# Updating the recurrent states of eight samples in three GpSimd operations in place of ScalarE and VectorE

## The chip, the core and the metric

The kernel runs on one core of one Trainium2 chip. The metric is device time in microseconds (us) of one execution. Before the change it is 1835.34 us, the median of three runs (1832.19 to 1837.56). Five engines work at once, each through its own instructions in order: TensorE (PE in the profile; PEld is its weight loading), VectorE (DVE), ScalarE (ACT), GpSimd (POOL) and SyncE (SP). DMAs are issued by SP, ACT and POOL and move data beside them.

## The reference

One layer of a decoder is computed for a prompt of 256 tokens and for eight single new tokens (the "samples"), which stand together as 264 columns. It has a mixer of three branches (spatial gating, HGRN2 and GLA), an output projection and an MLP, in float32. What the change touches is the recurrence of the two linear-attention branches, for a sample a single step:

```python
S = exp(log_f) * S + k v^T      # per sample and head
o = S^T q
```

HGRN2 has 8 heads with states of 128x128, GLA 4 heads with states of 128x256, and each of the eight samples has states of its own, read from memory, updated, used for `o` and written back as outputs.

## The kernel before

All large matrix products go through the same stream. A weight block of four k-tiles by 256 columns (a "granule", 512 KB) is loaded by a DMA on SP's queue into `raw`; in two halves of 128x512 ScalarE rounds it into `whi` (line 109) and VectorE takes the remainder `wlo = raw - whi` (line 106); PE then runs three products for each 128x128 tile (lines 659, 660 and 661: high weights with high and low inputs, low weights with high inputs). `whi` and `wlo` have six buffers each, which is the granule in work and two ahead. PE's list therefore needs two halves of ScalarE's and of VectorE's work for each granule, and both engines can run a little ahead of it.

Everything else of the mixers is written as generators that are advanced a little after each granule (`background`). The order of PE's, POOL's (and, in part of the program, SP's) instructions is that of the program text; VectorE's and ScalarE's orders are put together by a planner when the program is built.

The sample states are the work of `samples_r`, called once for each of three groups: two halves of HGRN2 (group 0 and 1, four heads each, one step for each sample, so 8 steps) and GLA (group 2, two heads to a step, so 16 steps). The 32 steps lie between 357 and 817 us of the span. A step holds 128 partitions by 512 elements. In the loop over the steps n:

- POOL's queue issues the fetch of the state of step n+2 (line 1077, tile `st`, four buffers) and the fetch of the values v of step n+1, spread over all partitions (line 1083, tile `vbc`, two buffers).
- ScalarE multiplies the state by the decay, one head at a time because the factor is a value for each partition and head (line 1103).
- VectorE adds k times v, again one head at a time (line 1105).
- POOL's queue issues the store of the new state (line 1106).
- Once all heads of a sample are there, PE forms `o` from the states (line 686) at a later place in its list; this is also what frees the `st` buffers, so a fetch waits for PE's use of the state two steps back.

Two other items share POOL's queue: line 1134 writes the values of a group to memory before its steps, and line 1254 stores the prompt's final states when VectorE has them ready.

Of the kernel before, what the change touches and what calls it, by code (L numbers as in the profile page):

```python
# [10 lines left out]
AF = mybir.ActivationFunctionType  # L11
ALU = mybir.AluOpType
# [3 lines left out]
P = 128  # L16
D = 2048
KT = D // P
NP = 256
# [38 lines left out]
def hybrid_step_kernel(  # L58
# [8 lines left out]
    nc = tc.nc  # L67
    V, S, T = nc.vector, nc.scalar, nc.tensor
# [17 lines left out]
    def blk(shape=None, dt=F32):  # L86
        shape = shape or [P, 4, NT]
        return blkp.tile(shape, dt, tag="b", name=nm("b"))
# [4 lines left out]
    def tmp(shape, tag, bufs=2):  # L93
        return tp.tile(shape, F32, tag=tag, name=nm(tag), bufs=bufs)
# [4 lines left out]
    def mul(o, a, b):  # L99
        V.tensor_tensor(o, a, b, op=ALU.mult)  # L100
# [106 lines left out]
    def rstd_small(ms, scale, out):  # L207

        n, w = out.shape
        xx, aa = tmp([P, 16], "sx")[0:n, 0:w], tmp([P, 16], "sa")[0:n, 0:w]  # L210
        c = 0
        for m in ms if isinstance(ms, list) else [ms]:
            V.tensor_scalar(xx[:, c:c + m.shape[1]], m, scale, EPS, ALU.mult, ALU.add)
            c += m.shape[1]
        V.tensor_scalar(out.bitcast(I32), xx.bitcast(I32), -0.5, 1597463007.0, ALU.mult, ALU.add)
        for _ in range(3):
            mul(aa, out, out)
            V.scalar_tensor_tensor(aa, aa, -0.5, xx, ALU.mult, ALU.mult)
            V.scalar_tensor_tensor(out, aa, 1.5, out, ALU.add, ALU.mult)
# [842 lines left out]
    def samples_r(G):  # L1062

        dv = G.dv
        nj, nh = dv // P, 512 // dv
        q, k, g = G.q, G.k, G.g
        fs = tmp([P, 4, NS], "fs")
        S.activation(fs, g[:, :, NP:NT], AF.Exp)
        qm = blk([P, 4, NS, 32])
        mul(qm, q[:, :, NP:NT].unsqueeze(3).to_broadcast([P, 4, NS, 32]),  # L1070
            delta.rearrange("p (b c) -> p b c", b=NS).unsqueeze(1).to_broadcast([P, 4, NS, 32]))
        steps = [(b, h) for b in range(NS) for h in range(0, 4, nh)]
        ahead, vals = [], []

        def fetch(b, h):
            st = tmp([P, nh, dv], "st", ST_BUFS)
            nc.gpsimd.dma_start(st, G.s_in(b, h, nh))
            ahead.append((st, now[0]))

        def values(b, h):  # L1080
            v = tmp([P, 4, P], "vbc", VB_BUFS)
            r0 = 4 * nj * b + h * nj
            nc.gpsimd.dma_start(v, vs_d[G.i, r0:r0 + 4, :].partition_broadcast(P))
            vals.append((v.rearrange("p (h j) v -> p h (j v)", h=nh), now[0]))

        for s in steps[0:2]:
            fetch(*s)
            yield
        values(*steps[0])
        yield  # L1090
        os_ = tmp([P, dv], f"os{G.i}", 1)
        sts = []
        for n, (b, h0) in enumerate(steps):
            if n + 2 < len(steps):

                yield lambda: len(sts) + sum(len(x[3]) for x in samples) <= ST_BUFS - 3
                fetch(*steps[n + 2])
            if n + 1 < len(steps):
                values(*steps[n + 1])
            yield lambda: now[0] >= max(ahead[0][1] + FETCHED, vals[0][1] + FETCHED - 1)  # L1100
            st, v = ahead.pop(0)[0], vals.pop(0)[0]
            for i in range(nh):
                S.activation(st[:, i, :], st[:, i, :], AF.Copy, scale=fs[:, h0 + i, b:b + 1])  # L1103
            for i in range(nh):
                V.scalar_tensor_tensor(st[:, i, :], v[:, i, :], k[:, h0 + i, NP + b:NP + b + 1], st[:, i, :], ALU.mult, ALU.add)  # L1105
            nc.gpsimd.dma_start(G.s_out(b, h0, nh), st)  # L1106
            sts.append(st)
            if h0 + nh == 4:
                samples.append((now[0], (G, qm, os_), b, sts))
                sts = []  # L1110
            yield
        yield lambda: not samples
        yield READY
        ss, rr = tmp([P, 1], "sss", 1), tmp([P, 1], "srr", 1)
        S.activation(tmp([P, dv], "vt"), os_, AF.Square, accum_out=ss)
        rstd_small(ss, 1.0 / dv, rr)
        S.activation(os_, os_, AF.Copy, scale=rr)
        G.os = os_
        yield

    def mixer_r(G):
# [18 lines left out]
        q, k, g = G.q, G.k, G.g  # L1140

        bs.g.append(samples_r(G))


# [616 lines left out]
```

## Time and profile before

| | |
|---|---|
| median of three runs | 1835.34 us (1832.19 to 1837.56) |
| the profiled execution | 1832.18 us, of which the span of its instructions is 1830.4 us |
| PE busy | 1788.7 us, 98% of the span |
| PEld busy | 1696.5 us, 93% |
| VectorE busy | 1181.8 us, 65% |
| ScalarE busy | 1000.3 us, 55% |
| GpSimd busy, DMA issues counted | 131.3 us, 7% |
| ScalarE's part of the updates, line 1103 | 37.1 us in 96 instructions |
| VectorE's part of the updates, line 1105 | 34.2 us in 96 instructions |

A row of a group of instructions gives its line, its engine, what it writes and reads, how often, the busy time, the mean of one in nanoseconds, and behind the bar the time that the engine stood idle just before these instructions, with what ended it. A row of the timeline gives start, duration, engine and line, and in brackets the idle time before it. In a table of windows each row is a stretch of the span with the busy time of each engine in it. Matmuls are pipelined and the profile models their ends, so PE's busy share says little by itself; it is the idle time in front of PE's rows that tells where it had to wait.

### The profile page before, as it was taken

The numbers are of one execution on the slowest core, as the hardware profiler recorded it, in microseconds if no ns is written. First come the engines' busy times: TensorE is split into PE (matmuls) and PEld (weight loads), VectorE is DVE, ScalarE is ACT, GpSimd is POOL, SyncE is SP. The second block draws the span as 40 slices with busy tenths as digits, with TensorE's granted clock in tenths as the row PEclk, the third lists the DMA queues.
The fourth block names the chain that finished last, engine by engine and source line by source line (L and its number), as shares of the span: only waits on it lengthen the run. The fifth ranks groups of instructions, "written<-read, shape, count | busy, mean of one in ns | idle before, by whom it ended". The sixth has DMA issues, their size and how long they took to land.

```text
span 1830.4 us, 42186 instructions
## 1 busy us (share of the span) xinstructions
PE 1788.7 (98%) x17012; PEld 1696.5 (93%) x17012; DVE 1181.8 (65%) x2092; ACT 1000.3 (55%) x1818; POOL 131.3 (7%) x210
## 2 busy tenths in 40 slices
PE   6999999999999999999999999999999999999998
PEld 4889999989988999989999989999999999999997
DVE  4566677787576696566555667555666666666666
ACT  5544364666755765654445666555554545454544
POOL 4221000111111101210000000000000000000000
PEclk9999999999999999999999999999999999999999
DMA  9999697788787788897987964777666666666663
GB/s 326 354 343 304 195 304 231 215 266 276 239 287 233 229 270 278 274 323 250 308 254 265 327 180 146 246 256 227 191 197 194 197 194 196 195 195 196 196 196 106
DMA packets 330179, 442.05 MB, mean 242 GB/s; under 512 B 14946, under 2 KB 276944, under 8 KB 329984
## 3 DMA queue, kind: packets, MB, share of 16 engines
q1 hardware_dynamic: 311728, 380.26, 65.0%
q0 software_dynamic: 17184, 57.85, 9.1%
q8 instruction: 133, 2.18, 0.5%
q10 hardware_dynamic: 1072, 1.25, 0.2%
q14 instruction: 62, 0.51, 0.1%
HBM read 427.60 MB, written 11.70 MB: 240 GB/s over the span
## 4 chain that ended last, share of the span: by engine, by line
PE 88%; DMA 2%; DVE 2%; issue 1%; ACT 1%; POOL 0%; DVEq 0%; ACTq 0%; POOLq 0%
PE mm L659 27%; PE mm L661 26%; PE mm L660 26%; PE ada L376 3%; DMA vbc<-vs_d 1%; PE ada L308 1%; DVE wlo L106 1%; PE sm L851 1%; PE sm L1208 1%; PE sm L679 1%; PE sm L686 1%; DMA raw<-in_w_in_dram 0%; DVE b L106 0%; PE sm L1578 0%; ACT whi L109 0%
## 5 line engine op out<-in xcount | busy, mean ns | idle before, releaser
L659 PE MATMUL mm<-b,whi 128*128 128x264 f32 x4624 | 1292.4, 279 | 12.3 <-issue 5.1
L661 PE MATMUL mm<-b,wlo 128*128 128x264 f32 x4624 | 1279.7, 277 | 5.1 <-DVE wlo L106 4.5
L660 PE MATMUL mm<-b,whi 128*128 128x264 f32 x4624 | 1278.8, 277 | 0.8 <-DVE b L106 0.7
L106 DVE TENSOR_TENSOR wlo<-raw,whi 128x512 fp32r<-128x512 f32 x1136 | 774.4, 689 | 489.1 <-ACT whi L109 475.0
L109 ACT CAST whi<-raw 128x512 fp32r<-128x512 f32 x1136 | 691.8, 616 | 644.5 <-DVE wlo L106 331.7
L659 PEld LDWEIGHTS mm<-b,whi 128*128 128x128 f32 x4624 | 875.8, 189 | 53.0 <-issue 28.0
L661 PEld LDWEIGHTS mm<-b,wlo 128*128 128x128 f32 x4624 | 876.2, 189 | 7.3 <-DVE wlo L106 7.2
L660 PEld LDWEIGHTS mm<-b,whi 128*128 128x128 f32 x4624 | 876.2, 189 | 4.4 <-issue 3.0
L103 DVE TENSOR_TENSOR b<-b,mm 128x528 f32<-128x528 f32 (+1 forms) x137 | 95.7, 699 | 24.5 <-PE mm L661 13.0
L1105 DVE SCALAR_TENSOR_TENSOR st<-vbc,b,st 128x128 f32<-128x128 f32 (+1 forms) x96 | 34.2, 390 | 55.2 <-DMA vbc<-vs_d 50.4
L1103 ACT ACTIVATE st<-st,fs 128x128 f32<-128x128 f32 (+1 forms) x96 | 37.1, 430 | 50.5 <-DMA st<-in_state_hgrn_dram 26.9
L488 POOL DMA_DIRECT2D b<-in_w_ada_dram x64 | 46.2, 724 | 126.0 <-PE ada L308 94.4
L376 PE MATMUL ada<-araw,cT 128*32 128x512 f32 x296 | 39.8, 601 | 0.0
L308 PE MATMUL ada<-b,cT 128*32 128x256 f32 (+1 forms) x640 | 35.1, 356 | 2.8 <-DMA b<-in_w_ada_dram 2.6
L100 DVE TENSOR_TENSOR b<-b,b 128x512 f32<-128x512 f32 (+1 forms) x47 | 33.9, 741 | 1.3 <-ACT b L1221 1.0
L1106 POOL DMA_DIRECT2D out_dram<-st x32 | 23.6, 736 | 130.5 <-DVE st L1105 130.5
L308 PEld LDWEIGHTS ada<-b,cT 128*32 128x32 f32 x640 | 17.8, 113 | 14.9 <-DMA b<-in_w_ada_dram 6.2
L376 PE MATMUL ada<-b,cT 128*32 128x512 f32 x216 | 26.2, 594 | 0.0
L106 DVE TENSOR_TENSOR b<-gt,b 128x528 fp32r<-128x528 f32 x32 | 22.7, 710 | 3.2
L106 DVE TENSOR_TENSOR b<-b 128x1024 f32<-128x1024 f32 (+1 forms) x24 | 24.3, 1017 | 0.0
L1632 ACT ACTIVATE b<-vt 128x528 fp32r<-128x528 f32 x32 | 23.0, 719 | 1.0
L106 DVE TENSOR_TENSOR b<-b,b 128x1056 fp32r<-128x1056 f32 (+3 forms) x21 | 20.8, 991 | 4.0 <-ACT b L109 3.8
(344 smaller groups left out, 854.0 us busy)
## 6 DMA issues: line engine op xcount, KB each, us to landing
raw<-in_w_in_dram SPq DMA_DIRECT2D x231, 512.0 KB, 4.8
raw<-in_w_mlp_up_dram SPq DMA_DIRECT2D x128, 512.0 KB, 3.9
raw<-in_w_mlp_down_dram SPq DMA_DIRECT2D x128, 512.0 KB, 3.7
araw<-in_w_ada_dram SPq DMA_DIRECT2D x74, 512.0 KB, 5.7
b<-in_w_ada_dram SPq DMA_DIRECT2D x54, 512.0 KB, 6.6
b<-in_w_ada_dram POOLq DMA_DIRECT2D x48, 512.0 KB, 8.9
raw<-in_w_branch_dram SPq DMA_DIRECT2D x48, 512.0 KB, 4.5
raw<-in_w_out_dram SPq DMA_DIRECT2D x32, 512.0 KB, 5.3
```

The costliest lines, as they stand in the source:

```text
L100: V.tensor_tensor(o, a, b, op=ALU.mult)
L103: V.tensor_tensor(o, a, b, op=ALU.add)
L106: V.tensor_tensor(o, a, b, op=ALU.subtract)
L109: S.copy(hi, src)
L308: T.matmul(acc[32 * j:32 * j + 32, 0:n], cT[:, k, :], w[:, n * j:n * j + n], start=k == 0, stop=k == KT - 1)
L376: T.matmul(self.acc[32 * j:32 * j + 32, :], cT[:, k, :], ws[j // 2][:, j % 2 * 512:j % 2 * 512 + 512], start=k == 0, stop=k == KT - 1)
L488: queue.dma_start(w[:, i], w1[k * P:(k + 1) * P, :, self.k0 * P:(self.k0 + self.n) * P])
L659: T.matmul(o, a, xh(k + j), start=first and j == 0, stop=False)
L660: T.matmul(o, a, xl(k + j), start=False, stop=False)
L661: T.matmul(o, b, xh(k + j), start=False, stop=last and j == n - 1)
L1103: S.activation(st[:, i, :], st[:, i, :], AF.Copy, scale=fs[:, h0 + i, b:b + 1])
L1105: V.scalar_tensor_tensor(st[:, i, :], v[:, i, :], k[:, h0 + i, NP + b:NP + b + 1], st[:, i, :], ALU.mult, ALU.add)
```

## The change

The per-head loops on ScalarE and VectorE become three GpSimd operations over the whole step of 128x512: the state times the decay, the values times k (in place in `vbc`), and their sum into the state. The per-partition factors are read as operands spread along the free dimension. The fetches before and the store after them stay where they are in the text.

```diff
             st, v = ahead.pop(0)[0], vals.pop(0)[0]
-            for i in range(nh):
-                S.activation(st[:, i, :], st[:, i, :], AF.Copy, scale=fs[:, h0 + i, b:b + 1])
-            for i in range(nh):
-                V.scalar_tensor_tensor(st[:, i, :], v[:, i, :], k[:, h0 + i, NP + b:NP + b + 1], st[:, i, :], ALU.mult, ALU.add)
+            wide = [P, nh, dv]
+            nc.gpsimd.tensor_tensor(st, st, fs[:, h0:h0 + nh, b:b + 1].to_broadcast(wide), op=ALU.mult)
+            nc.gpsimd.tensor_tensor(v, v, k[:, h0:h0 + nh, NP + b:NP + b + 1].to_broadcast(wide), op=ALU.mult)
+            nc.gpsimd.tensor_tensor(st, st, v, op=ALU.add)
             nc.gpsimd.dma_start(G.s_out(b, h0, nh), st)
             sts.append(st)
```

In the built program PE's list is the same, row for row. VectorE and ScalarE lose 96 instructions each and keep the rest nearly in the old order; POOL's list gains 96, and reads for each step: fetch of state n+2, fetch of values n+1, the three operations of step n, store of step n.

## The prediction

> **What bounds the kernel now.** I read the page's busy times and chain first, then the groups of the two lines that go.
>
> ```profile
> span 1830.4 us, 42186 instructions
> PE 1788.7 (98%) x17012; PEld 1696.5 (93%) x17012; DVE 1181.8 (65%) x2092; ACT 1000.3 (55%) x1818; POOL 131.3 (7%) x210
> ...
> PE 88%; DMA 2%; DVE 2%; issue 1%; ACT 1%; POOL 0%; DVEq 0%; ACTq 0%; POOLq 0%
> ...
> L106 DVE TENSOR_TENSOR wlo<-raw,whi 128x512 fp32r<-128x512 f32 x1136 | 774.4, 689 | 489.1 <-ACT whi L109 475.0
> ...
> L1105 DVE SCALAR_TENSOR_TENSOR st<-vbc,b,st 128x128 f32<-128x128 f32 (+1 forms) x96 | 34.2, 390 | 55.2 <-DMA vbc<-vs_d 50.4
> L1103 ACT ACTIVATE st<-st,fs 128x128 f32<-128x128 f32 (+1 forms) x96 | 37.1, 430 | 50.5 <-DMA st<-in_state_hgrn_dram 26.9
> ```
>
> The chain that ended last is PE for 88%: its list of products sets the time. VectorE and ScalarE feed it with `wlo` and `whi`, and the lines that go are not on the chain. What they take is visible all the same: VectorE spends 34.2 us in line 1105 and stands 55.2 us in front of it, mostly for the values' DMA, with `wlo` instructions queued behind. So the question is what PE loses to late operands between 380 and 817 us. I cut that stretch where PE takes states or a group begins, and asked for each window's busy times; the last row is the sum over eleven adjoining windows.
>
> ```profile
> core 0: us, PE busy (x) PEld busy (x) DVE busy (x) ACT busy (x) POOL busy (x), PEclk, DMA share, GB/s
> ...
> 408.00:460.00 52.00, 52.00 (x591) 48.38 (x584) 38.48 (x76) 32.85 (x68) 10.20 (x15) 1.00 0.87 284
> ...
> 545.00:575.00 30.00, 26.90 (x405) 24.52 (x404) 22.45 (x46) 19.11 (x41) 5.72 (x9) 0.94 0.77 251
> ...
> 640.00:685.00 45.00, 42.80 (x594) 40.76 (x593) 40.56 (x65) 29.50 (x54) 4.96 (x8) 0.96 0.85 277
> 685.00:722.00 37.00, 37.00 (x449) 34.42 (x449) 28.18 (x50) 21.96 (x45) 7.97 (x12) 1.00 0.88 293
> ...
> 757.00:817.00 60.00, 57.31 (x514) 52.51 (x507) 35.11 (x71) 33.45 (x69) 13.99 (x21) 1.00 0.92 314
> sum 437.00, PE 426.42 PEld 395.58 DVE 303.82 ACT 276.69 POOL 66.18; mean PE 38.77 PEld 35.96 DVE 27.62 ACT 25.15 POOL 6.02
> ```
>
> PE is idle 10.6 us here (437.0 less 426.4). That is all that could be won in this stretch, 0.6% of the span.
>
> **The change part by part.**
>
> *What goes, and what it can win.* The timeline gives the places where PE waited for a `wlo`, and VectorE's wait just before each.
>
> ```profile
> 397.29 0.88 DVE L1105 SCALAR_TENSOR_TENSOR st<-vbc,b,st 128x128 f32<-128x128 f32 x3 [5.10 <-DMA vbc<-vs_d]
> ...
> 519.78 0.61 DVE L1105 SCALAR_TENSOR_TENSOR st<-vbc,b,st 128x128 f32<-128x128 f32 x2 [6.05 <-DMA vbc<-vs_d]
> ...
> 781.87 0.88 DVE L1105 SCALAR_TENSOR_TENSOR st<-vbc,b,st 128x256 f32<-128x256 f32 x2 [7.36 <-DMA vbc<-vs_d]
> ...
> 805.81 0.88 DVE L1105 SCALAR_TENSOR_TENSOR st<-vbc,b,st 128x256 f32<-128x256 f32 x2 [3.32 <-issue]
> ```
> ```profile
> 398.83 0.38 PE L661 MATMUL mm<-b,wlo 128*128 128x264 f32 x1 [0.53 <-DVE wlo L106]
> ...
> 521.67 0.38 PE L661 MATMUL mm<-b,wlo 128*128 128x264 f32 x1 [0.68 <-DVE wlo L106]
> ...
> 786.99 0.38 PE L661 MATMUL mm<-b,wlo 128*128 128x264 f32 x1 [0.43 <-DVE wlo L106]
> ...
> 807.34 0.38 PE L661 MATMUL mm<-b,wlo 128*128 128x264 f32 x1 [2.26 <-DVE wlo L106]
> ```
>
> VectorE stood 5 to 7 us three times for the values, and PE lost 0.5 to 0.7 us each time: the buffers ahead cover the rest. With lines 1103 and 1105 gone these three go: 0.53 + 0.68 + 0.43 = 1.6 us. The fourth, 2.26 us, stood behind a gap of VectorE that no DMA or engine ended, so I don't count it as won, but it may go too. Gain 1.6 us, with 0 and 10.6 us as ends. The 71 us of busy time that ScalarE and VectorE get back (37.1 + 34.2) win nothing beyond that, because PE is the bound.
>
> *What is added on POOL.* No row of before is a GpSimd operation of 128x512. The nearest are those of 128x128 and 128x32 around 1095 and 1101 us.
>
> ```profile
> 1094.89 0.44 POOL L1533 TENSOR_TENSOR gs<-gs,nr 128x128 f32<-128x128 f32 x1 [1.27 <-DVE nr L233]
> 1095.41 0.46 POOL L1534 TENSOR_TENSOR xsT<-xsT,gs 128x128 f32<-128x128 f32 x1
> ...
> 1100.13 0.25 POOL L1565 TENSOR_TENSOR b<-xsn,b 128x32 fp32r<-128x32 f32 x1
> ...
> 1100.81 0.21 POOL L1564 CAST b<-xsn 128x32 fp32r<-128x32 f32 x1
> ...
> 1101.30 0.47 POOL L1564 CAST b<-xsn 128x32 fp32r<-128x32 f32 x1
> ```
> ```profile
> 1101.28 0.43 DVE L106 TENSOR_TENSOR b<-vt,b 128x256 fp32r<-128x256 f32 x1 [0.50 <-ACT b L109]
> ```
>
> From 32 to 128 elements the time rises from 0.25 to 0.45 us, 2.1 ns an element, so 512 elements take 0.45 + 384 x 0.0021 = 1.25 us, and the start of the next comes 0.07 us after an end (1094.89 + 0.44 to 1095.41, rounded down). I use 1.31 us an operation and 3.94 us for the three of a step; over 32 steps that is 126 us of POOL. The floor of one operation is 0.45 us, that of a quarter of its size; the ceiling four of those, 1.8 us. I take the line between, because the three sizes lie on one.
>
> *What POOL and VectorE take from each other.* The cast of 128x32 takes 0.21 us, but 0.47 us where it starts 0.02 us behind a VectorE operation with two inputs, and it ends with that one (1101.77 against 1101.71 us). So the two engines don't run such work side by side. The Trainium skill, "SBUF — State Buffer", section "Who interferes with whom", says that a VectorE instruction with two SBUF inputs and a GpSimd instruction that reads SBUF exclude each other for the whole of the one that came first. By that rule the trace agrees in this one pair, 0.47 against 0.21 us; taken for every microsecond of POOL's work it makes the sum the upper end below, 8.8 us, and by what the trace shows of the cover ahead of PE it makes 1.6. The price for VectorE has two ends. It is nothing if `wlo` is far enough ahead, and at most the whole of POOL's time, if every microsecond of it stops VectorE. For the upper end I take each window's VectorE time, less line 1105, plus 3.94 us for each step that falls there.
>
> ```profile
> 408.00:460.00 52.00, 6.11 (x20) 1.00 0.87 284
> ...
> 545.00:575.00 30.00, 3.65 (x12) 0.94 0.77 251
> ...
> 640.00:685.00 45.00, 2.73 (x6) 0.96 0.85 277
> 685.00:722.00 37.00, 3.68 (x8) 1.00 0.88 293
> ...
> 757.00:817.00 60.00, 6.41 (x14) 1.00 0.92 314
> ```
>
> These rows are line 1105 alone. By POOL's new order the windows hold 6, 3, 2, 4 and 8 steps: 38.5 - 6.1 + 23.6 = 56.0 of 52 us; 22.5 - 3.7 + 11.8 = 30.6 of 30; 40.6 - 2.7 + 7.9 = 45.7 of 45; 28.2 - 3.7 + 15.8 = 40.3 of 37; 35.1 - 6.4 + 31.5 = 60.2 of 60. The excess is 4.0 + 0.6 + 0.7 + 3.3 + 0.2 = 8.8 us, and it would be PE's. But VectorE is only stopped while it has something to run, about three quarters of the time in the two worst windows (38.5 of 52, 28.2 of 37); with 0.75 of POOL's time they come to 50.1 of 52 and 36.3 of 37, and nothing is left over. For windows that full the row 640 to 685 is the nearest: VectorE is busy 40.6 of 45 us there and PE loses 2.2. I put 0.8 us on each of the two, 1.6 us together, between 0 and 8.8.
>
> *What now waits on POOL's queue.* The three operations of step n stand behind the fetch of n+2, which waits until PE has used a state two steps back; before, only DMAs stood there. ScalarE and VectorE did the update as soon as the data were in. So PE's wait for a state is new. The tightest places are the ends of group 0 and of group 2, where the last steps come in a row.
>
> ```profile
> 439.85 0.75 POOL L1077 DMA_DIRECT2D st<-in_state_hgrn_dram  x1 [11.35 <-PE sm L686]
> ...
> 790.61 0.72 POOL L1077 DMA_DIRECT2D st<-in_state_gla_dram  x1 [6.84 <-PE sm L686]
> 791.32 0.57 POOL L1083 DMA_DIRECT2D vbc<-vs_d  x1
> 791.88 0.71 POOL L1106 DMA_DIRECT2D out_dram<-st  x1
> ```
> ```profile
> 460.52 1.26 PE L686 MATMUL sm<-st,b 128*32 128x128 f32 x20
> ...
> 816.18 0.64 PE L686 MATMUL sm<-st,b 128*32 128x256 f32 x8
> ```
>
> With U for the three operations of a step: from 790.61 POOL issues a fetch and the values (to 791.9), then U, a store, a fetch and values (2.0), U, a store and values (1.3), U, a store (0.7), U: the last state is ready at 795.9 + 4U, and PE takes it at 816.18. So U may be 5.07 us. In group 0 the same sum from 439.85 (a fetch, values; U; store, values; U; store; U) gives 443.2 + 3U against 460.52, U up to 5.8 us. Alone U is 3.94; if each operation first waits for a whole `wlo` of 0.69 us it is 6.0. I let it wait for VectorE's busy share of the last window, 35.1 of 60: 0.59 x 0.69 = 0.41, so U = 5.17 and PE waits 4 x 0.10 = 0.4 us. The ends are 0 (U = 3.94) and 4 x 0.93 + 3 x 0.2 = 4.3 us. Other groups of steps have more room. Line 1254's store, which waits for VectorE, now holds updates up too; the next use is far enough off that I put nothing on it. The fetches issued behind an update leave up to 5 us later and are needed a whole step after that, and On SP's queue two weight loads change places with two others, which I put at nothing.
>
> *The sum.* Against the profiled execution's own 1832.18 us: -1.6 + 1.6 + 0.4 = +0.4, 1832.6 us. That execution lay 3.2 us under the median of the runs, 1835.34, so the median comes to 1835.7, say 1836 us: no change that this kernel's measurement can tell (0.3%, 5.5 us).
>
> **The rivals.**
>
> *Slower through VectorE.* POOL's 126 us stop VectorE whenever it holds the port; `wlo` comes late in the full windows, and PE waits for line 106. For it speaks the one pair of rows above, against it that waits of 5 to 7 us cost PE only 0.5 to 0.7. It decides when the stopped share of POOL's time passes about 0.83 (52 less 32.4, over 23.6). Price: the 8.8 us, without the 1.6 and with 0.4 for the states: 1835.3 + 7.6 = 1843 us.
>
> *Slower through the states.* POOL's operations take longer than the line through three small sizes gives, or VectorE always goes first, so that U is 7.4 us (1.31 plus 1.15 an operation, nearly two `wlo` each). PE waits 4 x 2.3 at 816 and 3 x 1.6 at 460, 14 us, and some less at other uses: 1835.3 + 14 = 1849 us, up to 1853. It decides from U = 5.07. The Trainium skill, "GPSIMD Engine Reference", section "Engine selection", advises VectorE for elementwise work because two-input operations are about twice as slow on GpSimd. No run here shows a GpSimd operation of this size yet.
>
> *Faster.* The waits for DMAs leave both feeding engines, the fourth `wlo` wait goes too, and the port costs nothing: -1.6 - 2.3, and some of the remaining 6.7 us of PE's idle time if its cause is a late `whi`: -4 to -8, 1828 to 1831 us. Against it: part of PE's idle time ends in nothing that the profile names.
>
> **How the numbers follow.** No change to tell: 0.42 (its own range 1830 to 1841). Slower through VectorE 0.23 and through the states 0.15, together 0.38. Faster by over 5.5 us: 0.20. The range of 1829 to 1850 us leaves out half of the faster case and the worst of the states case, some 0.2.
>
> **What would show it.** Lines 1103 to 1105 on POOL with about 1.3 us each, a little more where VectorE is busy. Line 106 with a mean above its 689 ns, or idle time before it, between 380 and 817 us. No wait of ScalarE or VectorE for `st` or `vbc`. PE's idle sum in these windows near 10.6 us; a wait of PE for POOL at the last line 686 of group 2, if anywhere. The prediction is wrong if operations of 128x512 take 2 us or more, if PE waits for line 106 for more than 5 us there, or if PE's idle sum halves.

## The result, and the profile after

The changed kernel takes 1841.88 us, the median of five runs (1839.12 to 1842.03), against 1833.96 us for the kernel before, also of five (1832.19 to 1837.56). The ratio is 1.0037 with a 95% interval of 1.0023 to 1.0051: slower by 7.9 us by the medians, by 6.8 us by the ratio. A few single executions of over 3100 us in the experiments below are left out of all medians and ratios, and from the one trace that was taken of such an execution, with twice GpSimd's reads, only GpSimd's own times are read. The time lies in the forecast's range (1829 to 1850 us), 5.9 us above its number and just outside the likeliest case's own range of 1830 to 1841. Nearest to it is the rival "slower through VectorE", 1843 us.

The page of the kernel after, its span, busy times and chain, and the groups that answer to those shown of before:

```profile
span 1837.3 us, 42020 instructions
PE 1789.7 (97%) x17012; PEld 1697.0 (92%) x17012; DVE 1235.9 (67%) x1996; ACT 973.3 (53%) x1722; POOL 264.2 (14%) x306
...
PE 89%; DVE 2%; ACT 1%; issue 1%; DVEq 0%; ACTq 0%
...
L106 DVE TENSOR_TENSOR wlo<-raw,whi 128x512 fp32r<-128x512 f32 x1136 | 827.0, 737 | 498.0 <-ACT whi L109 485.6
...
L1105 POOL TENSOR_TENSOR st<-st,vbc 128x512 f32<-128x512 f32 x32 | 51.9, 1620 | 2.5
L1103 POOL TENSOR_TENSOR st<-st,fs 128x512 f32<-128x512 f32 x32 | 43.5, 1361 | 20.7 <-ACT fs L1068 20.3
...
L1104 POOL TENSOR_TENSOR vbc<-vbc,b 128x512 f32<-128x512 f32 x32 | 37.5, 1173 | 2.2 <-DMA vbc<-vs_d 2.2
```

POOL works 132.9 us in the three lines. VectorE has 96 instructions fewer, 34.2 us of work given away, and is busy 54 us longer (1235.9 against 1181.8): the remaining ones take longer, line 106 737 ns in place of 689. Two stretches of the timeline of the kernel after show how, first VectorE's rows, then POOL's.

```profile
378.04 0.66 DVE L106 TENSOR_TENSOR wlo<-raw,whi 128x512 fp32r<-128x512 f32 x1
378.62 3.88 DVE L106 TENSOR_TENSOR b<-b 128x1024 f32<-128x1024 f32 x1
382.43 1.75 DVE L106 TENSOR_TENSOR wlo<-raw,whi 128x512 fp32r<-128x512 f32 x1
384.10 1.21 DVE L106 TENSOR_TENSOR b<-b 128x1024 f32<-128x1024 f32 x1
...
547.60 4.19 DVE L100 TENSOR_TENSOR b<-b,b 128x512 f32<-128x512 f32 x2
```
```profile
379.35 1.06 POOL L1103 TENSOR_TENSOR st<-st,fs 128x512 f32<-128x512 f32 x1
380.36 1.05 POOL L1104 TENSOR_TENSOR vbc<-vbc,b 128x512 f32<-128x512 f32 x1
381.49 2.14 POOL L1105 TENSOR_TENSOR st<-st,vbc 128x512 f32<-128x512 f32 x1
383.93 0.80 POOL L1106 DMA_DIRECT2D out_dram<-st  x1 [0.29 <-POOL st L1105]
...
547.49 1.06 POOL L1103 TENSOR_TENSOR st<-st,fs 128x512 f32<-128x512 f32 x1
548.50 1.05 POOL L1104 TENSOR_TENSOR vbc<-vbc,b 128x512 f32<-128x512 f32 x1
549.63 1.60 POOL L1105 TENSOR_TENSOR st<-st,vbc 128x512 f32<-128x512 f32 x1
```

A VectorE operation of 128x1024 takes 1.21 us undisturbed (384.10) and 3.88 us where POOL's operations begin beside it; the `wlo` behind it takes 1.75 in place of 0.66. At 547.60 two operations of line 100 take 4.19 us over a whole burst of POOL. What this does to PE, in rows of PE's timeline and its waits from 355 to 830 us (wait, its sum, how often, the longest), again of the kernel after:

```profile
384.23 0.59 PE L661 MATMUL mm<-b,wlo 128*128 128x264 f32 x1 [3.02 <-DVE wlo L106]
...
551.93 1.08 PE L679 MATMUL sm<-b 128*32 128x32 f32 x64 [3.14 <-DVE b L100]
```
```profile
PE mm L661 <- DVE wlo L106: 10.2, 7, 3.0
PE sm L679 <- DVE b L100: 3.1, 1, 3.1
PE mm L660 <- issue: 1.4, 1, 1.4
```

PE waits 13.3 us for VectorE (10.2 + 3.1), at 384 and 551 us right behind these bursts. It never waits for POOL.

To compare the stretch that ends with PE's last instruction of line 686 (816.18 + 0.64 us before), here are windows from 380 us to that end, with busy times, granted clock, DMA share and GB/s as the last columns. The first fence is the kernel after, the second the kernel before.

```profile
380.00:824.00 444.00, 428.70 (x4796) 396.75 (x4795) 355.49 (x481) 256.50 (x494) 191.69 (x189) 0.99 0.81 263
384.20:386.00 1.80, 1.77 (x8) 1.77 (x9) 1.80 (x3) 1.17 (x4) 0.52 (x1) 0.50 0.43 129
```
```profile
380.00:817.00 437.00, 426.42 (x4786) 395.58 (x4785) 303.82 (x579) 276.69 (x573) 66.18 (x99) 0.99 0.82 269
```

The windows end on whole microseconds. The stretch is 7.0 us longer, as much as the whole span (1837.3 less 1830.4 is 6.9; the profiled execution of after took 1839.12 us, that of before 1832.18). PE's idle time in it rises from 10.6 to 15.3 us, 4.7 of the 7. The other 2.3 us are PE being busy longer with the same list (428.70 against 426.42). A part of them is clock: right behind the 3.02 us of idle time the granted clock is 0.50. Cut into windows of 2 us, PE's busy time times what the granted clock lacks to 1.00 comes to 4.5 us in this stretch and to 3.4 us in that of before, so an estimate of 1.1 of the 2.3 us; what the rest is stays open.

### The profile page after: what moved, and what is told of

The parts are those of the page before. It is cut to its first block, busy times and chain, and to the rows that moved or that the text cites. A ratio compares the mean times of both kernels' runs of the same rounds, so it can differ in the third digit from the quotient of the medians.

```text
span 1837.3 us, 42020 instructions
## 1 busy us (share of the span) xinstructions
PE 1789.7 (97%) x17012; PEld 1697.0 (92%) x17012; DVE 1235.9 (67%) x1996; ACT 973.3 (53%) x1722; POOL 264.2 (14%) x306
## 4 chain that ended last, share of the span: by engine, by line
PE 89%; DVE 2%; ACT 1%; issue 1%; DVEq 0%; ACTq 0%
PE mm L659 27%; PE mm L661 27%; PE mm L660 27%; PE ada L376 3%; PE ada L308 1%; DVE wlo L106 1%; PE sm L679 1%; PE sm L851 1%; PE sm L1208 1%; PE sm L686 1%; PE sm L1578 0%; DVE b L106 0%; DVE b L100 0%; ACT whi L109 0%; DVE b L1558 0%
## 5 line engine op out<-in xcount | busy, mean ns | idle before, releaser
L661 PE MATMUL mm<-b,wlo 128*128 128x264 f32 x4624 | 1281.7, 277 | 10.6 <-DVE wlo L106 10.4
L106 DVE TENSOR_TENSOR wlo<-raw,whi 128x512 fp32r<-128x512 f32 x1136 | 827.0, 737 | 498.0 <-ACT whi L109 485.6
L1105 POOL TENSOR_TENSOR st<-st,vbc 128x512 f32<-128x512 f32 x32 | 51.9, 1620 | 2.5
L1103 POOL TENSOR_TENSOR st<-st,fs 128x512 f32<-128x512 f32 x32 | 43.5, 1361 | 20.7 <-ACT fs L1068 20.3
L100 DVE TENSOR_TENSOR b<-b,b 128x512 f32<-128x512 f32 (+1 forms) x47 | 41.5, 911 | 0.4 <-ACT b L1221 0.3
L1104 POOL TENSOR_TENSOR vbc<-vbc,b 128x512 f32<-128x512 f32 x32 | 37.5, 1173 | 2.2 <-DMA vbc<-vs_d 2.2
L106 DVE TENSOR_TENSOR b<-b 128x1024 f32<-128x1024 f32 (+1 forms) x24 | 31.4, 1310 | 0.0
```

The costliest lines, as they stand in the source:

```text
L106: V.tensor_tensor(o, a, b, op=ALU.subtract)
L661: T.matmul(o, b, xh(k + j), start=False, stop=last and j == n - 1)
L1103: nc.gpsimd.tensor_tensor(st, st, fs[:, h0:h0 + nh, b:b + 1].to_broadcast(wide), op=ALU.mult)
L1105: nc.gpsimd.tensor_tensor(st, st, v, op=ALU.add)
```

## The experiments

Each was run five times or more beside the kernel before on the same chip. PE's list is the same in all but the one with later updates. Times of different chips are compared by their ratios to before.

### The update left out, and GpSimd's time spent on writes alone

```diff
-            (lines 1102 to 1105, ScalarE's and VectorE's loops)
+            (nothing)
```

> Left out: the update of the states (fetches, stores and PE's use of the states stay), so the outputs of the sample states and of the samples' recurrences are not the reference's. VectorE's and ScalarE's lists are those of the changed kernel but for a few rows, PE's list is the same. Port theory (GpSimd operations that read SBUF stop VectorE's operations with two inputs, and PE waits for wlo): without them the loss is gone and the updates' own waits too, so 2 to 5 us under before, 1829 to 1833 us. Order theory (the planner's new order of VectorE and ScalarE costs the time): as the changed kernel, about 1842 us. Queue theory (POOL's list is late with states and fetches): 1829 to 1833 as well.

Measured: 1818.41 us, ratio 0.9913 (0.9898 to 0.9928).

The second kernel of this pair has memsets in place of the two loops:

```diff
+            for q in range(4):
+                nc.gpsimd.memset(v, 0.0)
+            for q in range(4):
+                nc.gpsimd.memset(st, 0.0)
```

> Left out: the update; in its place eight GpSimd memsets of 128x512 a step, four on the values and four on the state, which write SBUF and read nothing and keep POOL busy for about 4 us a step, as the three operations do (outputs as in the run without updates). Port theory, read side: as without any update, 1829 to 1833 us, and the mean of line 106 between 355 and 820 us back at 0.69 us from 0.90. Queue theory: as the changed kernel, 1840 to 1842 us. If any GpSimd work stops VectorE, writing too: 1840 us or more, with line 106 at 0.85 us or more.

Measured: 1820.75 us, ratio 0.9924 (0.9911 to 0.9937). The groups of the two lines in this kernel, and `wlo` in it, from 355 to 830 and from 355 to 820 us:

```profile
L1103 POOL MEMSET vbc<- 128x512 f32 x128 | 67.8, 529 | 21.3 <-DMA vbc<-vs_d 15.7
L1105 POOL MEMSET st<- 128x512 f32 x128 | 67.1, 524 | 5.5
```
```profile
L106 DVE TENSOR_TENSOR wlo<-raw,whi 128x512 fp32r<-128x512 f32 x273 | 185.0, 689 | 128.9 <-ACT whi L109 126.9 <-PE sm L686 1.3
```

The same group, 355 to 820 us, in the kernel without the update and then in the kernel after:

```profile
L106 DVE TENSOR_TENSOR wlo<-raw,whi 128x512 fp32r<-128x512 f32 x273 | 184.2, 689 | 131.2 <-ACT whi L109 129.3 <-PE sm L686 1.3
```
```profile
L106 DVE TENSOR_TENSOR wlo<-raw,whi 128x512 fp32r<-128x512 f32 x256 | 222.6, 895 | 71.8 <-ACT whi L109 70.3 <-PE sm L686 0.7 <-PE mm L661 0.3
```

Two things follow. First, POOL's queue and the new order aren't what costs: with 134.9 us of POOL's time at the places of the three operations, and VectorE's and ScalarE's lists but for a few rows those of the change, the kernel is 2.3 us slower than without the update, with intervals that overlap. What the memsets don't do is read SBUF; `wlo` keeps its 689 ns beside them and takes 895 beside the changed kernel's operations. The Trainium skill, "SBUF — State Buffer", section "Who interferes with whom", says that a VectorE instruction with two SBUF inputs contends with a GpSimd instruction that reads SBUF and not with one that only writes it. The trace agrees on both halves: 895 and 689 ns. The memsets are also shorter pieces, 0.53 us each against 1.05 us and more; reads in pieces of that length were not run.

Second, the update of the kernel before cost 16.0 us (1834.38 less 1818.41), not the 1.6 us of the prediction, and more than the 2 to 5 us expected of this run. On the scale of this chip the changed kernel is at 1.0037 x 1834.38 = 1841.2 us, 22.8 us over the kernel without an update.

The stretch to PE's last line 686, in the kernel without the update:

```profile
380.00:803.00 423.00, 420.83 (x4790) 392.04 (x4790) 278.04 (x482) 255.43 (x490) 63.44 (x95) 1.00 0.83 274
```

It is 14 us shorter than in before. PE is idle 2.2 us in place of 10.6, that is 8.4 us, and busy 5.6 us less with the same list (420.83 against 426.42). Against after it is 21 us: 13.1 idle and 7.9 busy.

### Twice GpSimd's reads

```diff
             nc.gpsimd.dma_start(G.s_out(b, h0, nh), st)
+            nc.gpsimd.tensor_tensor(v, v, v, op=ALU.mult)
+            nc.gpsimd.tensor_tensor(v, v, v, op=ALU.mult)
```

(on the changed kernel)

> The changed kernel with two more GpSimd operations of 128x512 on the used values behind each store (some 3.2 us a step, reading SBUF; results stay). Port theory: what stops VectorE grows from 4 to about 7.3 us a step, so the loss against the run without updates grows by about 80%: if that loss is 10 us, 18 us, 1848 to 1852 us. Order theory: no further loss, about 1842 us. Queue theory: PE waits for POOL at the states, at the end of group 2 first, by 3 us a step in a row, 1845 to 1855 us, and the profile shows those waits at line 686.

Measured: 1882.36 us, ratio 1.026 (1.0243 to 1.0276), 41.2 us over the change's 1841.2. The 64 more operations take 77.3 us of GpSimd in this run's trace (33.7 and 43.6). The first 133 us of reads cost 22.8 us, 0.17 us for each; the next 77 cost 41.2, 0.53 for each. The time grows with the reads, and faster than they do. That the first ones use up what slack VectorE had would explain it. A later fetch or store behind POOL's longer queue would too, and no trace of this run shows which.

### The same change with its rows apart

```diff
-   POOL per step: fetch n+2, values n+1, decay n, product n, sum n, store n
+   POOL per step: values n+1, decay n, fetch n+2, product n, store n-1, sum n
```

> The changed kernel with POOL's list alone reordered: in each step the fetch of the state two steps on stands between the two products, and the store of the step before stands in front of the addition; the lists of PE, VectorE, ScalarE and SP stay row for row. The same 96 operations, 131 us, but a DMA issue of 0.6 to 0.8 us between each two. Row theory (GpSimd holds the port over operations that follow each other without a gap, so VectorE stands for several of them; single ones cost little): most of the loss goes, 1823 to 1831 us, and no operation of line 106 on 128x1024 takes over 2.6 us. Time theory (the loss is in proportion to POOL's reading time): as the changed kernel, 1840 to 1843 us.

Measured: 1849.23 us, ratio 1.0079 (1.0062 to 1.0096), slower still than the change. `wlo`, 355 to 820 us, of this kernel:

```profile
L106 DVE TENSOR_TENSOR wlo<-raw,whi 128x512 fp32r<-128x512 f32 x254 | 225.7, 914 | 65.4 <-ACT whi L109 64.3 <-PE sm L686 0.7
```

That three operations follow in a row isn't the cause: with, in most steps, a DMA issue of 0.5 to 0.8 us between them `wlo` takes 914 ns. Why the issues leave VectorE no gap, these runs don't show.

### Only the decay on GpSimd

```diff
-            for i in range(nh):
-                S.activation(st[:, i, :], st[:, i, :], AF.Copy, scale=fs[:, h0 + i, b:b + 1])
+            nc.gpsimd.tensor_tensor(st, st, fs[:, h0:h0 + nh, b:b + 1].to_broadcast(wide), op=ALU.mult)
             for i in range(nh):
                 V.scalar_tensor_tensor(...)
```

> Only the decay is on GpSimd (one operation of 1.05 us a step), the rest on VectorE as before; ScalarE is out. Port theory: a quarter of the stopping time, 34 us in all instead of 131, while line 1105's 34 us of VectorE and its waits for the values come back: between before and the changed kernel, 1834 to 1838 us. Order theory: lists differ from both, anything from 1834 to 1842 us. Queue theory: little of POOL's queue is used, 1834 us.

Measured: 1825.49 us, ratio 0.9953 (0.994 to 0.9966). This computes the reference and beats both kernels. POOL's operations take 44.3 us in place of 132.9, and `wlo` takes nearly its old time; VectorE still adds, but waits for less. By the starts and lengths of the rows, 25 of the 44 us fall where VectorE is busy, against 123 of 133 us in the kernel after. The group of `wlo` (355 to 820 us) and VectorE's waits (355 to 830 us) in this kernel, where line 1102 is the decay and 1104 the product and sum:

```profile
L106 DVE TENSOR_TENSOR wlo<-raw,whi 128x512 fp32r<-128x512 f32 x268 | 182.0, 696 | 63.8 <-ACT whi L109 61.7 <-PE sm L686 1.3
```
```profile
DVE st L1104 <- POOL st L1102: 29.6, 16, 3.3
DVE st L1104 <- DMA vbc<-vs_d: 9.4, 3, 3.9
```

VectorE stands 39 us for the update, at most 3.9 at once, against 55.2 and up to 7.4 before, and ScalarE no longer at all. For 29.6 of the 39 us it waits for POOL's decay, and the reads that fall there meet no operation of VectorE.

### The decay one step ahead

```diff
-            (decay of step n in front of VectorE's part)
+            (decay of step n+1 there; that of step 0 as well when n is 0)
```

(on the kernel with only the decay on GpSimd)

> The version meant to beat both: the decay on GpSimd as in the run with the decay alone there (1825.5 us), but one step ahead, before the store of the step in work, so that VectorE finds it done; the rest on VectorE as before. VectorE's waits for POOL, 30 us there, fall to under 10 us. If these waits still cost PE: 1820 to 1824 us. If not: 1824 to 1827 us.

Measured: 1839.75 us, ratio 1.0031 (1.0018 to 1.0045), 14 us slower than with the decay in its own step, and not the gain that was expected. VectorE's waits in this kernel (line 1104 is product and sum), 355 to 830 us:

```profile
DVE st L1104 <- DMA vbc<-vs_d: 56.3, 17, 8.7
```

With the decay done early, the planner put VectorE's line 1104 earlier, and VectorE stands 56.3 us for the values, up to 8.7 at once, as it did in before. POOL's decay also takes longer (51.4 us in all, 40 of them where VectorE is busy), `wlo` takes 709 ns, and PE waits 10.0 us for it against 2.1. So the better time above doesn't come from the ScalarE part alone. That it rests on VectorE coming to the update late is likely, but two things moved at once here.

### ScalarE's part alone, waiting and not waiting

```diff
             for i in range(nh):
                 S.activation(st[:, i, :], st[:, i, :], AF.Copy, scale=fs[:, h0 + i, b:b + 1])
-            for i in range(nh):
-                V.scalar_tensor_tensor(...)
```

> Left out: the product k v and its addition; only ScalarE's decay of the states stays, as in the kernel before (the outputs of the samples' recurrences are not the reference's). By the runs so far, ScalarE's part costs about 10 us and VectorE's about 6 of the 16 us that the updates cost in the kernel before: 1828 us here. If VectorE's part is the costly one: 1820 to 1822 us.

Measured: 1825.71 us, ratio 0.9955 (0.9937 to 0.9972).

```diff
+            dry = tmp([P, nh, dv], "vt")
             for i in range(nh):
-                S.activation(st[:, i, :], st[:, i, :], AF.Copy, scale=fs[:, h0 + i, b:b + 1])
+                S.activation(dry[:, i, :], cst[:, 0:dv], AF.Copy, scale=fs[:, h0 + i, b:b + 1])
-            (VectorE's loop)
```

> Left out: the update; ScalarE does as many activations of the same shapes as for the decay, but from a constant into a scratch tile, so none waits for a state's DMA (the states go out as they came). Wait theory (ScalarE's standing for the states' DMAs, with whi behind, is the cost): as without any update, 1818 to 1821 us. Work theory (its 37 us of busy time is the cost): as the run with the decay alone on ScalarE, 1826 to 1829 us.

Measured: 1819.04 us, ratio 0.9921 (0.9905 to 0.9936). ScalarE's waits in the first of the two, and its group in the second, 355 to 830 us:

```profile
ACT st L1103 <- DMA st<-in_state_gla_dram: 25.7, 10, 5.8
...
ACT st L1103 <- DMA st<-in_state_hgrn_dram: 15.4, 7, 4.6
```
```profile
L1104 ACT ACTIVATE vt<-cst,fs 128x128 f32<-128x128 f32 (+1 forms) x96 | 36.0, 428 | 0.2
```

By the ratios, the same 96 activations of 36 us cost 0.0008 or 1.5 us over the kernel without the update (0.9921 less 0.9913, with intervals that overlap) where they wait for nothing, and 0.0042 or 7.7 us where ScalarE stands 41 us for the states' DMAs. PE's waits in the first of the two, 355 to 830 us, show where it goes; neither row is there in the second, or without the update.

```profile
PE mm L661 <- DVE wlo L106: 2.2, 2, 2.0
...
PE mm L659 <- ACT whi L109: 1.0, 1, 1.0
```

For ScalarE's part it is the standing, with `whi` queued behind it, and not the work, that costs. It is 7.7 of the update's 16 us; VectorE's part was not run alone.

### The updates one granule later behind their fetches

```diff
-FETCHED = 3
+FETCHED = 4
```

> The kernel before with FETCHED = 4 in place of 3: each update is emitted one granule later behind its fetches, so the planner puts lines 1103 and 1105 later and they find their data there; nothing else is edited, and the busy time of the updates stays. Wait theory (what the updates cost in the kernel before, 16 us against no update, is VectorE's and ScalarE's standing for DMAs with wlo and whi queued behind): the 50 us of waits for the values fall to under 25 and the time by some 5 to 10 us, 1824 to 1829 us. Busy theory (it is the 71 us of work itself): no change, 1832 to 1836 us.

Measured: 1836.47 us, ratio 1.0002 (0.9994 to 1.0011). VectorE's wait for the values didn't fall (54.2 us against 50.4), ScalarE's for the states neither (53.8 against 43.8), so this run says nothing on what the waits cost.

### Other divisions of the three operations

Three more kernels compute the same with the work divided otherwise. Both products on ScalarE and the sum on VectorE in one instruction:

```diff
                 S.activation(st[:, i, :], st[:, i, :], AF.Copy, scale=fs[:, h0 + i, b:b + 1])
+                S.activation(v[:, i, :], v[:, i, :], AF.Copy, scale=k[:, h0 + i, NP + b:NP + b + 1])
+            V.tensor_tensor(st, st, v, op=ALU.add)
```

> No GpSimd operation: ScalarE does both products (state by decay, values by k, per head), VectorE one addition of 128x512 for a step. VectorE's part falls from 34 us to 32 x 0.69 = 22 us, ScalarE's doubles from 37 to about 74 us. Port theory: nothing to pay for. Wait theory: ScalarE now waits for both DMAs and VectorE for ScalarE, so about as the kernel before, 1830 to 1836 us. Busy theory: more work in sum, 1834 to 1840 us.

Measured: 1846.71 us, ratio 1.0047 (1.0032 to 1.0062). GpSimd computes nothing in it, and it is the second slowest of those that compute the whole without extra work: ScalarE now stands 63.9 us for DMAs (states 19.6 and 17.6, values 26.7), and PE waits 8.1 us for `wlo` and 6.3 for `whi`.

Both products on ScalarE, the sum on GpSimd (the edit is against the kernel just before):

```diff
-            V.tensor_tensor(st, st, v, op=ALU.add)
+            nc.gpsimd.tensor_tensor(st, st, v, op=ALU.add)
```

> ScalarE does both products, GpSimd only the addition with two full inputs (1.6 us a step, 52 us in all, against 131 in the change and 34 in the run with the decay alone). Port theory in proportion to POOL's reading time: 23 us x 52 / 131 = 9 us over the run without updates, 1827 us, and up to 8 us more for ScalarE's waits: 1827 to 1835 us. If one GpSimd operation at a time is harmless and only three in a row hurt, 1820 to 1825 us.

Measured: 1842.98 us, ratio 1.0035 (1.0021 to 1.0048). Here both costs meet: ScalarE stands 54.0 us for DMAs, and 42.2 us of GpSimd's reads bring `wlo` to 765 ns.

The decay on ScalarE, the second product on GpSimd, the sum on VectorE:

```diff
+            nc.gpsimd.tensor_tensor(v, v, k[:, h0:h0 + nh, NP + b:NP + b + 1].to_broadcast([P, nh, dv]), op=ALU.mult)
+            V.tensor_tensor(st, st, v, op=ALU.add)
```

> ScalarE does the decay as in the kernel before, GpSimd the product of values and k (1.05 us a step), VectorE one addition of 128x512 (0.69 us a step). POOL's reading time is that of the run with the decay on GpSimd (34 us), VectorE's own part is 22 us in place of 34, ScalarE's 37 us come back. Port and wait theory together: 1822 to 1829 us, within 4 us of the run with the decay on GpSimd (1825.5). If VectorE's own work counts most, under it by 3 us or more; if ScalarE's waits for the state's DMA count most, over it by 3 us or more.

Measured: 1836.89 us, ratio 0.9997 (0.9987 to 1.0006): no change. ScalarE stands 56.7 us for the states' DMAs, and 39.4 us of reads bring `wlo` to 737 ns. The same amount of GpSimd reading as in the decay alone (39.4 against 44.3 us) lengthens `wlo` more here, 737 against 696 ns, though about as much of it falls where VectorE is busy (23 us here, 25 there). Why is open.

## Why the prediction's number was near and its sum was wrong

*PE as the bound, and its idle time as all that could be won.* PE bounds all the kernels. But 10.6 us was not the ceiling: without the update the stretch is 14.0 us shorter, 8.4 us of it idle and 5.6 us "busy" time. In the kernel before, two stretches behind idle times ran at a lower granted clock, from 566 and from 679 us; windows of both, and the rows of PE in front of them:

```profile
566.00:568.00 2.00, 2.00 (x14) 2.00 (x14) 0.99 (x2) 1.60 (x4) 0.00 (x0) 0.67 0.96 345
568.00:570.00 2.00, 2.00 (x11) 2.00 (x11) 1.72 (x5) 1.98 (x6) 0.00 (x0) 0.50 0.43 135
...
680.00:682.00 2.00, 2.00 (x11) 2.00 (x11) 2.00 (x5) 0.52 (x1) 0.00 (x0) 0.50 0.63 174
```
```profile
565.89 0.27 PE L659 MATMUL mm<-b,whi 128*128 128x264 f32 x1 [2.86 <-issue]
...
678.16 0.38 PE L659 MATMUL mm<-b,whi 128*128 128x264 f32 x1 [2.19 <-issue]
678.38 0.28 PE L660 MATMUL mm<-b,whi 128*128 128x264 f32 x1
678.49 0.28 PE L661 MATMUL mm<-b,wlo 128*128 128x264 f32 x1
```
```profile
678.16 0.88 DVE L1105 SCALAR_TENSOR_TENSOR st<-vbc,b,st 128x256 f32<-128x256 f32 x2 [4.44 <-DMA vbc<-vs_d]
678.95 0.68 DVE L106 TENSOR_TENSOR wlo<-raw,whi 128x512 fp32r<-128x512 f32 x1
```

By the windows of 2 us the lower clock makes 3.4 of the 5.6 us, an estimate; without the update no window is under 0.97. The other 2.2 us stay open.

*The gain, -1.6 us: the term that failed first.* It was counted from three rows in which PE waits for `wlo` behind VectorE's wait for the values. It was 16.0 us. PE's idle time names two parts, here first in the kernel before and then without the update:

```profile
PE mm L659 <- issue: 5.1, 2, 2.9
PE mm L661 <- DVE wlo L106: 4.3, 5, 2.3
```
```profile
PE mm L659 <- issue: 1.6, 1, 1.6
```

The waits for `wlo` go, all five of them, and of the "issue" time, which I counted as nobody's, 3.5 us go with the lower clock behind it. One of these two idle times, 2.19 us, ended as VectorE's 4.44 us for the values ended, at 678.16. That doesn't mean that PE waited for VectorE: it goes on with line 659, which takes `whi`, and is at line 661 before VectorE's next `wlo` begins at 678.95. What the trace has in this gap is a transfer of 16 KB on the instruction queue, from 675.88 to 676.86 us (the transfers from 675.8 to 678.2 us of the kernel before: packets, MB, share):

```profile
q8 instruction: 1, 0.02, 2.6%
```

The traces of before, of after and of all the experiments but the one with twice the reads have 15 "issue" idle times of PE of 1 us or more between 380 and 826 us. Each ends 1.2 to 1.6 us after the end of such a transfer. So PE most likely stood for its own instructions there. Some 38 such transfers lie in that stretch of each kernel, and nearly all pass without such an idle time; why PE stands longer at them with the update in place, no run shows.

ScalarE's standing, 50.5 us in front of line 1103, had no term at all; alone, in the run with ScalarE's decay only, it cost 7.7 us. So "the buffers ahead cover the rest" does not hold for ScalarE. That both engines stand for the same steps, so that one uses up what the other has ahead, would explain it, but no run shows that by itself.

*GpSimd's operations, 1.31 us each and U = 3.94 us: near.* The three take 1361, 1173 and 1620 ns in the mean, 4.15 us a step; undisturbed ones take 1.05, 1.05 and about 1.3. The line through three small sizes gave the right size, but not that the three differ.

*VectorE stopped, +1.6 us with 8.8 as upper end: the term that failed second.* Measured 22.8 us, or 20.5 over the memsets. The mechanism was the right one, the size too small by more than ten times. It was set by whole windows, as though VectorE had to fall behind over 37 or 52 us before PE loses anything. But a burst stops VectorE for 3 us at once, PE waits 3.0 and 3.1 us right there, and the clock then adds its part. One of the prediction's own signs of being wrong came true: PE waits for line 106 for more than 5 us (10.2).

*The states, +0.4 us: nothing.* PE never waits for POOL. The rival "slower through the states" falls.

*The fourth `wlo` wait, 2.26 us behind a gap that nothing ended.* It was not counted as won. Without the update PE's whole idle time in the stretch is 2.2 us, so it went as well.

*The rivals.* "Slower through VectorE" named the mechanism, and its 1843 us is 1 us off; yet it reached that by 8.8 us of loss, 0.4 for the states and 1.6 of gain, where the runs show some 23 us of loss and 16 of gain. The "faster" rival was right that the DMA waits leave both feeding engines and that most of PE's unnamed idle time goes (5.1 us before, 1.4 after), and wrong that the port costs nothing. The number of the forecast was near by luck: two large terms of opposite sign, each taken at a tenth of its size or less, cancel for the greater part.

What stays open: which share of the 16 us is VectorE's standing alone, and which is PE's "issue" time and the clock behind it. The first was tried with later updates, which didn't shorten the waits; the 14 us between the decay in its step and one step ahead speak for it, but there POOL's times moved too.

## What to carry to other kernels

An engine that feeds the bound and stands for a DMA, with feeding work queued behind it, can cost far more than its own busy time suggests (7.7 us for 36 us of ScalarE's work that cost 1.5 without the standing): measure it by leaving the step out, or by the same instructions on data that is always there. Moving work to GpSimd frees such an engine, but here GpSimd's reads stopped VectorE's operations with two inputs for whole bursts (3.88 us for one of 1.21), so move the operation that waits and as little reading as does it: the decay alone, 44 us on GpSimd in place of 133, made 1825.5 us of 1834.4. Where PE is the bound, look at the granted clock behind each idle time of 2 us or more: it can add to its price.

## What the runs showed of the hardware that was not expected

- Idle times of PE of 2.19, 2.86 and 3.02 us were followed by a granted clock of 0.50 (windows above: 680 to 682 and 568 to 570 us before, 384.2 to 386 after). In before the matmuls start 0.22 us apart in place of 0.11 from 679.4 to 682.7 us, so that wait cost some 1.6 us more than its own length, an estimate. The Trainium skill, "TensorE: Matmul & The Clock Gate", section "HAM oscillation — how this bites in real kernels", puts the limit at about 3.4 us of idle time; here 2.2 us was enough. It isn't always: behind the 2.26 us at 807.34 in the kernel before (shown in the prediction) the clock stays at 1.00.

```profile
807.30:809.30 2.00, 1.96 (x17) 1.96 (x18) 2.00 (x4) 0.96 (x2) 0.42 (x1) 1.00 0.56 160
```

- The engine that is held up can stay so over more than one instruction of the other. One VectorE operation of 128x1024 lasts from 378.62 to 382.50 us, past two complete operations of POOL, though by the profile it had started 0.73 us ahead of the first; the rule quoted in the prediction, that the one that came first shuts the other out for its whole length, isn't what these rows show. The other way, this row of the kernel after shows a POOL operation of 1.06 us that takes 9.01 while VectorE runs operations with two inputs back to back; with the decay alone on GpSimd the same operation takes 8.99 us.

```profile
647.91 9.01 POOL L1103 TENSOR_TENSOR st<-st,fs 128x512 f32<-128x512 f32 x1 [2.00 <-ACT fs L1068]
```

- An operation of GpSimd on 128x512 with one operand spread along the free dimension takes 1.05 us, one with two full inputs (two different tiles) 1.28 us at the least and mostly 1.6 in the kernel after.
